# Weights split in two rings of twelve blocks instead of six pairs of blocks: a two-layer decoder trunk on one core

## The chip, the cores and the metric

The kernel runs on one core of one Trainium2 chip. The metric is the device time of one execution in microseconds (us); lower is better. Before the change it is 2327.83 us, the median of three runs (2327.59 to 2328.57).

The engines go by the profile's names: PE is TensorE (matmul; PEld is its weight load), DVE is VectorE, ACT is ScalarE, POOL is GpSimd, SP is SyncE, which issues most of the DMAs.

## The reference

256 tokens of width 2048 pass two pre-norm residual layers. Each layer is a token mixer (layer 0 an HGRN2 gated recurrence, layer 1 gated linear attention) beside a 4-head cross-attention into 256 memory tokens, an output projection, and a SwiGLU feed-forward network of width 5632. All of it is float32.

```python
for layer in range(DEPTH):                      # 2
    hn = _rmsnorm(h, norm_mix[layer])
    if layer % NUM_MIXERS == 0:
        y, xq = _hgrn2_mixer(hn, hgrn_w_in[j], lbs[j], hgrn_onorm[j])
    else:
        y, xq = _gla_mixer(hn, gla_w_in[j], gla_w_gk[j], gla_b_gk[j], gla_onorm[j])
    xa = _memory_attention(xq, mem_n, w_mem_kv[layer])
    h = h + jnp.concatenate([y, xa], axis=-1) @ w_out[layer]
    hn = _rmsnorm(h, norm_ffn[layer])
    gate, up = jnp.split(hn @ w_gate_up[layer], 2, axis=-1)
    h = h + (jax.nn.silu(gate) * up) @ w_down[layer]
return _rmsnorm(h, norm_final)
```

## The kernel before

**Products in two parts.** A float32 factor is split into a high part in the type that the matmul takes (fp32r) and a low part, the rest. A product is three matmuls into one PSUM bank: high x high, high x low, low x high (lines 249 to 251 and 333 to 335). The weights come from memory as float32 and are split on the fly, a block of 128 x 512 at a time: ScalarE copies the block to the high part (line 207), VectorE subtracts the high part from the block and writes the low part (line 208).

**Buffers.** `new_raw` gives one of 4 raw tiles of four blocks (tag "raw"). `split` takes one of 6 tiles of the tag "parts"; each holds the high and low parts of up to two blocks. It is called with one or two blocks. A tile is given back when the last matmul that reads it is done.

**Projections.** `project` walks over quads of 128-row strips of the weights. For each quad `weights` issues one DMA of up to 1 MB and splits it two blocks at a time; then 24 matmuls follow (four strips, two tiles of 128 tokens, three matmuls). The first quad of the program is loaded and split block by block. `step()` places pieces of other work, such as transposes, between the strips.

**Feed-forward.** `ffn` computes gate and up in 11 blocks of 512 columns each (`up_block`), and lays parts of the down projection between them, two `down` calls after each block. `project_halves` does a block: eight pairs of strips, and for each pair a 2 x 2 problem of blocks b00, b01, b10, b11 (strip by half). The kinds of pairs are S, O and H:

- S takes seven products instead of eight. It splits b00, then b11 and b10 together; VectorE forms sums and differences of blocks in place in the raw tile (lines 350 to 352: one instruction of two blocks, two of one); the four results t5, t7 and t6, t4 are split two and two. That makes four tiles of "parts": a (one block), b, c and d (two each). The products go in the order 1, 3, 2, 5, 7, 6, 4. 21 matmuls.
- O takes eight products, 24 matmuls, from two tiles of two blocks.
- H takes eight products; it forms one difference (line 366) and splits it alone, three tiles in all.

Blocks 0 to 2 of a layer have the pairs SHOSHOSO, SHOSSOSO and SHOSSOSO, the other eight SSOSSOSS. After the eighth pair a copy (line 828), additions (line 831), SiLU (line 833) and a product (line 834) follow.

**Order.** Each engine runs its instructions in one order, fixed when the program is made: about that of the source, but an instruction that is found ready early may be put ahead of one that has to wait. Waits between engines go by the part of a tile that is read or written.

**Other tenants.** The keys and values of the cross-attention of both layers (`kv0`, `kv1`), and in layer 1 the reloaded `kv` and the gate's weights and low-rank inputs (`gk`), each take a "parts" tile through `side`.

Of the kernel before, what the change touches and what calls it, by code (L numbers as in the profile page):

```python
# [35 lines left out]
def trunk_kernel(ctx: ExitStack, tc: tile.TileContext, x, mem, norm_mix, norm_ffn, norm_mem,  # L36
# [156 lines left out]
    def side(shape, name):  # L193
        return wts.tile(shape, F32, tag="parts", name=name, bufs=6)

# [5 lines left out]
    def split(src, name, by=2):  # L201

        n, m = src.shape[1:]
        both = wts.tile([P, 2, 2, 512], F32R, tag="parts", name=f"parts{name}", bufs=6)
        for k in range(0, n, by):
            j = min(k + by, n)
            nc.scalar.copy(out=both[:, 0, k:j, 0:m], in_=src[:, k:j, :])  # L207
            nc.vector.tensor_tensor(out=both[:, 1, k:j, 0:m], in0=src[:, k:j, :],  # L208
                                    in1=both[:, 0, k:j, 0:m].bitcast(F32), op=ALU.subtract)
        return [(both[:, 0, k, 0:m], both[:, 1, k, 0:m]) for k in range(n)]  # L210

    def weights(w, k0, nk, c0, n):
# [5 lines left out]
        return [p for k in range(0, nk, 2) for p in split(raw[:, k:k + 2, 0:n], f"{i}_{k}", 1 if i == 0 else 2)]  # L218
# [102 lines left out]
    def project_halves(forms, kinds, w, c0, c1, name):  # L321
# [15 lines left out]
        for p, kind in enumerate(kinds):  # L337
            i, raw = new_raw()

            for j, c in ((slice(0, 4, 3), c0), (slice(1, 3), c1)):  # L340
                nc.sync.dma_start(out=raw[:, j, :],
                                  in_=w[2 * p * P:(2 * p + 2) * P, c:c + 512].rearrange("(k p) c -> p k c", p=P))
            x = forms[p].get
            last = p == len(PAIRS) - 1
            if kind == "S":
                tt = nc.vector.tensor_tensor
                b00, = split(raw[:, 0:1, :], f"{i}a")
                b11, b10 = split(raw[:, 2:4, :], f"{i}b")

                tt(out=raw[:, 0:2, :], in0=raw[:, 0:4:2, :], in1=raw[:, 1:2, :].broadcast_to([P, 2, 512]), op=ALU.subtract)  # L350
                tt(out=raw[:, 2, :], in0=raw[:, 2, :], in1=raw[:, 0, :], op=ALU.add)  # L351
                tt(out=raw[:, 3, :], in0=raw[:, 3, :], in1=raw[:, 2, :], op=ALU.subtract)  # L352
# [108 lines left out]
    kv_out = away.tile([P, 2, XH * T], F32, name="kv_out")  # L461
    later(lambda: nc.scalar.dma_start(out=kv_out, in_=kv))


    def attention(l, ps, r, yq):
# [35 lines left out]
        def turn_probs(m):  # L501
            pT = st["pT", m] = work.tile([P, XH, T], F32, tag=("T", "sc")[m], name=f"pT{l}{m}")
# [260 lines left out]
    def gla(hq, r, yq):  # L763
        w = gla_w_in[0]
        half = (GR + XA) // 2
        kv = side([P, 2, XH * T], "kv")
        nc.scalar.dma_start(out=kv, in_=kv_out)
        kT[1] = kv[:, 0, :].rearrange("p (h t) -> p h t", t=T)
        vm[1] = kv[:, 1, :].rearrange("p (m c) -> p m c", c=XA)
        gk = side([P, 6, T], "gk")  # L770
        wgk = gk[:, 0:4, :]
# [14 lines left out]
        def decay(pr):  # L786
# [3 lines left out]
            for a in range(2):  # L790
                hd = 2 * pr + a
                zp = aux_ps(f"zp{hd}")
                for j in range(2):
                    nc.tensor.matmul(zp[:, j * T:(j + 1) * T], wgk[:, hd, j * P:(j + 1) * P], lowT,
                                     start=True, stop=True)
# [160 lines left out]
```

## Time and profile before

| | |
|---|---|
| median of 3 runs | 2327.83 us |
| the profiled execution | 2328.0 us |
| its span, first to last instruction | 2326.2 us |
| granted TensorE clock | 0.999 |
| busy share PE / DVE / ACT / POOL | 99% / 81% / 54% / 1% |
| DMA | 435.51 MB, mean 187 GB/s |
| feed-forward stage, layer 0 | 544.4 to 1248.1 us |
| feed-forward stage, layer 1 | 1615.9 to 2316.9 us |

The profile is of one execution. The span is shorter than the execution's time by 1.8 us. Matmuls are pipelined and their ends are modelled, so a busy PE isn't PE at its peak; start-to-start times of matmuls say how fast it goes. Instructions of VectorE and ScalarE overlap a little too: the next one can start before the time of the one ahead of it is over, so that start-to-start times are what counts there as well. In a timeline row stand the start, the time, the engine, the line, the operation with output and inputs, and in brackets how long the engine sat idle before it and who released it. The number in a name such as parts152c is the raw tile's number, the letter that of the split.

### The profile page before, as it was taken

To read this page: it belongs to the slowest core of one execution; us is meant where nothing else is said; L and a number is where in the kernel's file an instruction comes from. 1 tells how busy PE (TensorE), PEld (TensorE's weight loads), DVE (VectorE), ACT (ScalarE), POOL (GpSimd) and SP (SyncE) were. 2 spreads that over 40 slices of the span, in tenths; PEclk is the share of its full clock that TensorE was granted. 3 is DMA by queue.
4 is the path that set the end of the run, shared out by engine and by line. 5 is a ranking of instruction groups with operands and counts; after the bars stand their busy time and mean duration, and the time that the engine had idled before them with its cause. 6 is when DMAs were issued, how large, how long until landed. Compare 5 with 4: busy or idle time off the path is not lost.

```text
span 2326.2 us, 28901 instructions
## 1 busy us (share of the span) xinstructions
PE 2303.5 (99%) x11034; PEld 1940.7 (83%) x11034; DVE 1888.0 (81%) x2262; ACT 1261.2 (54%) x1643; POOL 22.2 (1%) x39
## 2 busy tenths in 40 slices
PE   9999999999999999999999999999999999999998
PEld 7888888888887888888889999988887888888886
DVE  5565565668999999999985664557999999999995
ACT  7543535356555655555555654356555555555563
POOL 0000000000000000000000000000000000000000
PEclk9999999999999999999999999999999999999999
DMA  8554445454556555556565445455465656656563
GB/s 315 193 172 159 163 145 181 136 190 164 198 181 214 196 188 202 196 202 209 187 226 166 150 147 167 152 198 174 166 214 189 208 183 209 205 186 213 200 217 127
DMA packets 229211, 435.51 MB, mean 187 GB/s; under 512 B 10028, under 2 KB 38992, under 8 KB 228816
## 3 DMA queue, kind: packets, MB, share of 16 engines
q1 hardware_dynamic: 227776, 429.40, 54.8%
q10 hardware_dynamic: 1296, 4.26, 0.5%
q8 instruction: 86, 1.41, 0.2%
q14 instruction: 53, 0.43, 0.1%
HBM read 430.48 MB, written 3.15 MB: 186 GB/s over the span
## 4 chain that ended last, share of the span: by engine, by line
PE 63%; DVE 26%; issue 6%; ACT 4%; DMA 0%; ACTq 0%; DVEq 0%; POOLq 0%; SPq 0%
PE f_p L334 4%; PE f_p L335 4%; PE f_p L333 4%; DVE raw L350 4%; DVE parts L208 4%; PE fd L250 3%; PE fd L251 3%; PE fd L249 3%; PE wo L251 3%; PE wo L249 3%; PE wo L250 2%; DVE raw L351 2%; DVE raw L352 2%; PE slh L578 1%; PE hgate L249 1%
## 5 line engine op out<-in xcount | busy, mean ns | idle before, releaser
L208 DVE TENSOR_TENSOR parts<-raw,parts 128x1024 fp32r<-128x1024 f32 (+3 forms) x490 | 557.7, 1147 | 290.8 <-ACT parts L207 289.9
L207 ACT CAST parts<-raw 128x1024 fp32r<-128x1024 f32 (+3 forms) x490 | 476.8, 991 | 430.4 <-PE wo L251 64.4
L350 DVE TENSOR_TENSOR raw<-raw 128x1024 f32<-128x1024 f32 x118 | 143.7, 1217 | 0.2
L351 DVE TENSOR_TENSOR raw<-raw 128x512 f32<-128x512 f32 x118 | 81.6, 692 | 3.9
L352 DVE TENSOR_TENSOR raw<-raw 128x512 f32<-128x512 f32 x118 | 81.6, 692 | 3.8
L414 DVE TENSOR_TENSOR h<-fd,h 128x512 f32<-128x512 f32 x94 | 61.9, 684 | 6.2 <-PE fd L251 6.0
L831 DVE TENSOR_TENSOR e<-f_p,e 128x512 f32<-128x512 f32 x66 | 44.9, 681 | 0.0
L833 ACT ACTIVATE s<-s,rf_r 128x512 f32<-128x512 f32 x44 | 31.8, 722 | 7.0 <-DVE s L831 7.0
L562 DVE COPY_PREDICATED sch<-mask,slh 128x512 f32<-128x512 uint8 x15 | 10.8, 722 | 28.4 <-PE slh L578 28.4
L834 DVE SCALAR_TENSOR_TENSOR s<-e,rf_r,s 128x512 f32<-128x512 f32 x44 | 32.3, 741 | 0.0
L578 PEld LDWEIGHTS slh<-Q,K 128*128 128x128 f32 x240 | 29.1, 191 | 1.2
L831 DVE TENSOR_TENSOR s<-f_p,e 128x512 f32<-128x512 f32 x44 | 29.5, 683 | 0.0
L578 PE MATMUL slh<-Q,K 128*128 128x64 f32 x240 | 28.4, 271 | 0.0
L249 PE MATMUL wo<-parts,y_3h 128*128 128x512 f32 x64 | 25.9, 405 | 0.0
L249 PE MATMUL wo<-parts,y_0h 128*128 128x512 f32 x64 | 25.7, 402 | 0.0
L250 PE MATMUL fd<-parts,s_5h 128*128 128x512 f32 x64 | 25.4, 397 | 0.0
L250 PE MATMUL fd<-parts,s_7h 128*128 128x512 f32 x64 | 25.4, 396 | 0.0
L250 PE MATMUL fd<-parts,s_1h 128*128 128x512 f32 x64 | 25.3, 396 | 0.0
L249 PE MATMUL fd<-parts,s_2h 128*128 128x512 f32 x64 | 25.3, 396 | 0.0
L249 PE MATMUL fd<-parts,s_4h 128*128 128x512 f32 x64 | 25.3, 396 | 0.0
L249 PE MATMUL fd<-parts,s_6h 128*128 128x512 f32 x64 | 25.3, 396 | 0.0
L249 PE MATMUL fd<-parts,s_8h 128*128 128x512 f32 x64 | 25.3, 396 | 0.0
(5486 smaller groups left out, 7401.6 us busy)
## 6 DMA issues: line engine op xcount, KB each, us to landing
raw<-in_w_gate_up_dram SPq DMA_DIRECT2D x352, 512.0 KB, 4.0
raw<-in_w_down_dram SPq DMA_DIRECT2D x88, 1024.0 KB, 4.9
raw<-in_hgrn_w_in_dram SPq DMA_DIRECT2D x52, 1024.0 KB, 5.0
raw<-in_gla_w_in_dram SPq DMA_DIRECT2D x48, 768.0 KB, 4.3
raw<-in_w_out_dram SPq DMA_DIRECT2D x32, 1024.0 KB, 4.9
raw<-in_w_mem_kv_dram SPq DMA_DIRECT2D x15, 1024.0 KB, 8.2
raw<-in_gla_w_in_dram SPq DMA_DIRECT2D x8, 528.0 KB, 3.7
mtok<-in_mem_dram SPq DMA_DIRECT2D x4, 512.0 KB
```

The costliest lines, as they stand in the source:

```text
L207: nc.scalar.copy(out=both[:, 0, k:j, 0:m], in_=src[:, k:j, :])
L208: nc.vector.tensor_tensor(out=both[:, 1, k:j, 0:m], in0=src[:, k:j, :], in1=both[:, 0, k:j, 0:m].bitcast(F32), op=ALU.subtract)
L249: nc.tensor.matmul(acc, xh, hi[:, o:o + m], start=first, stop=False)
L250: nc.tensor.matmul(acc, xh, lo[:, o:o + m], start=False, stop=False)
L251: nc.tensor.matmul(acc, xl, hi[:, o:o + m], start=False, stop=last)
L333: nc.tensor.matmul(ps[b], xh, hi, start=first, stop=False)
L334: nc.tensor.matmul(ps[b], xh, lo, start=False, stop=False)
L335: nc.tensor.matmul(ps[b], xl, hi, start=False, stop=left[b] == 0)
L350: tt(out=raw[:, 0:2, :], in0=raw[:, 0:4:2, :], in1=raw[:, 1:2, :].broadcast_to([P, 2, 512]), op=ALU.subtract)
L351: tt(out=raw[:, 2, :], in0=raw[:, 2, :], in1=raw[:, 0, :], op=ALU.add)
L352: tt(out=raw[:, 3, :], in0=raw[:, 3, :], in1=raw[:, 2, :], op=ALU.subtract)
L578: nc.tensor.matmul(ps, st["K"][:, f, t * P:(t + 1) * P], q, start=i == 0, stop=i == len(parts) - 1)
```

## The change

The six "parts" tiles give way to two tiles that are allocated once: `part_h` with the high parts and `part_l` with the low parts of twelve blocks each. `split` takes places in them in turn, round and round, and takes as many neighbouring blocks at once as it is given, so one VectorE instruction writes the low parts of up to four blocks; at the end of the ring it breaks in two. ScalarE's copies still take two blocks (three for the first split of an S pair). The capacity in blocks is what the six tiles had.

For an S pair there are now two splits, of three and of four blocks, where there were four. The raw tile's blocks lie in another order (b00, b11, b10, b01), a pair is loaded by three DMAs instead of two, and the products go 1, 3, 2, 5, 6, 4, 7. An O pair and a quad of `weights` are one split of four. Keys, values and gate inputs move from "parts" tiles to tiles of the "work" pool.

```diff
-        both = wts.tile([P, 2, 2, 512], F32R, tag="parts", name=f"parts{name}", bufs=6)
-        for k in range(0, n, by):
-            j = min(k + by, n)
-            nc.scalar.copy(out=both[:, 0, k:j, 0:m], in_=src[:, k:j, :])
-            nc.vector.tensor_tensor(out=both[:, 1, k:j, 0:m], in0=src[:, k:j, :],
-                                    in1=both[:, 0, k:j, 0:m].bitcast(F32), op=ALU.subtract)
-        return [(both[:, 0, k, 0:m], both[:, 1, k, 0:m]) for k in range(n)]
+    NB = 12
+    part_h = wts.tile([P, NB, 512], F32R, name="part_h")
+    part_l = wts.tile([P, NB, 512], F32R, name="part_l")
+    at = [0]
+    def split(src, by=2):
+        n, m = src.shape[1:]
+        pairs = []
+        k = 0
+        while k < n:
+            i = at[0] % NB
+            j = min(n - k, NB - i, n if by > 1 else 1)
+            at[0] += j
+            hi, lo, s = part_h[:, i:i + j, 0:m], part_l[:, i:i + j, 0:m], src[:, k:k + j, :]
+            for c in range(0, j, by):
+                d = min(c + by, j)
+                nc.scalar.copy(out=hi[:, c:d, :], in_=s[:, c:d, :])
+            nc.vector.tensor_tensor(out=lo, in0=s, in1=hi.bitcast(F32), op=ALU.subtract)
+            pairs += [(hi[:, c, :], lo[:, c, :]) for c in range(j)]
+            k += j
+        return pairs
...
-        return [p for k in range(0, nk, 2) for p in split(raw[:, k:k + 2, 0:n], f"{i}_{k}", 1 if i == 0 else 2)]
+        return split(raw[:, 0:nk, 0:n], 1 if i == 0 else 2)
...
-            for j, c in ((slice(0, 4, 3), c0), (slice(1, 3), c1)):
-                nc.sync.dma_start(out=raw[:, j, :],
-                                  in_=w[2 * p * P:(2 * p + 2) * P, c:c + 512].rearrange("(k p) c -> p k c", p=P))
+            lo, hi = [w[(2 * p + k) * P:(2 * p + k + 1) * P, :] for k in range(2)]
+            nc.sync.dma_start(out=raw[:, 0:4:2, :],
+                              in_=w[2 * p * P:(2 * p + 2) * P, c0:c0 + 512].rearrange("(k p) c -> p k c", p=P))
+            nc.sync.dma_start(out=raw[:, 1, :], in_=hi[:, c1:c1 + 512])
+            nc.sync.dma_start(out=raw[:, 3, :], in_=lo[:, c1:c1 + 512])
...
             if kind == "S":
                 tt = nc.vector.tensor_tensor
-                b00, = split(raw[:, 0:1, :], f"{i}a")
-                b11, b10 = split(raw[:, 2:4, :], f"{i}b")
-                tt(out=raw[:, 0:2, :], in0=raw[:, 0:4:2, :], in1=raw[:, 1:2, :].broadcast_to([P, 2, 512]), op=ALU.subtract)
-                tt(out=raw[:, 2, :], in0=raw[:, 2, :], in1=raw[:, 0, :], op=ALU.add)
-                tt(out=raw[:, 3, :], in0=raw[:, 3, :], in1=raw[:, 2, :], op=ALU.subtract)
-                t5, t7 = split(raw[:, 0:2, :], f"{i}c")
-                t6, t4 = split(raw[:, 2:4, :], f"{i}d")
+                b00, b11, b10 = split(raw[:, 0:3, :], 3)
+                tt(out=raw[:, 0:4:3, :], in0=raw[:, 0:2, :], in1=raw[:, 3:4, :].broadcast_to([P, 2, 512]), op=ALU.subtract)
+                tt(out=raw[:, 1, :], in0=raw[:, 1, :], in1=raw[:, 0, :], op=ALU.add)
+                tt(out=raw[:, 2, :], in0=raw[:, 2, :], in1=raw[:, 1, :], op=ALU.subtract)
+                t5, t6, t4, t7 = split(raw)
...
-                for b in (1, 2, 6, 7, 5, 4, 3) if last else (1, 3, 2, 5, 7, 6, 4):
+                for b in (1, 2, 6, 7, 5, 4, 3) if last else (1, 3, 2, 5, 6, 4, 7):
                     product(b, x(todo[b][0]), todo[b][1])
             else:
-                b00, b01 = split(raw[:, 0:2, :], f"{i}a")
-                b11, b10 = split(raw[:, 2:4, :], f"{i}b")
+                b00, b11, b10, b01 = split(raw)
...
-                    nc.vector.tensor_tensor(out=raw[:, 3, :], in0=raw[:, 3, :], in1=raw[:, 2, :], op=ALU.subtract)
-                    e1, = split(raw[:, 3:4, :], f"{i}c")
+                    nc.vector.tensor_tensor(out=raw[:, 2, :], in0=raw[:, 2, :], in1=raw[:, 1, :], op=ALU.subtract)
+                    e1, = split(raw[:, 2:3, :])
...
-        kv = side([P, 2, XH * T], f"kv{l}")
-        kT.append(kv[:, 0, :].rearrange("p (h t) -> p h t", t=T))
-        vm.append(kv[:, 1, :].rearrange("p (m c) -> p m c", c=XA))
+        kT.append(work.tile([P, XH, T], F32, tag=("v", "F")[l], name=f"kT{l}"))
+        vm.append(work.tile([P, NT, XA], F32, tag=("gate", "K")[l], name=f"vm{l}"))
...
+    def put_away():
+        nc.scalar.dma_start(out=kT_out, in_=kT[1])
+        nc.scalar.dma_start(out=vm_out, in_=vm[1])
...
-        kv = side([P, 2, XH * T], "kv")
-        nc.scalar.dma_start(out=kv, in_=kv_out)
...
+        kT[1] = work.tile([P, XH, T], F32, tag="v", name="kT")
+        nc.scalar.dma_start(out=kT[1], in_=kT_out)
+        vm[1] = work.tile([P, NT, XA], F32, tag="gate", name="vm")
+        nc.scalar.dma_start(out=vm[1], in_=vm_out)
+        both = work.tile([P, 3, T], F32, tag="sc", name="gk0")
+        wgk = [both[:, 0:2, :], work.tile([P, 2, T], F32, tag="scx", name="gk1")]
+        for pr in range(2):
+            nc.gpsimd.memset(wgk[pr], 0.0)
+            nc.sync.dma_start(out=wgk[pr][0:GR, :, 0:DK], in_=gla_w_gk[0][:, 2 * pr * DK:2 * (pr + 1) * DK].rearrange(
+                "r (h c) -> r h c", c=DK))
```

More of the change, by code (lines that the diff above doesn't have):

```diff
@@ L459, in trunk_kernel @@
             nc.scalar.activation(out=vm[l][:, t, :], in_=ps[t], func=AF.Copy, scale=rm[:, t:t + 1])
-    kv_out = away.tile([P, 2, XH * T], F32, name="kv_out")
-    later(lambda: nc.scalar.dma_start(out=kv_out, in_=kv))
+    kT_out = away.tile([P, XH, T], F32, name="kT_out")
+    vm_out = away.tile([P, NT, XA], F32, name="vm_out")
+    def put_away():
+        nc.scalar.dma_start(out=kT_out, in_=kT[1])
+        nc.scalar.dma_start(out=vm_out, in_=vm[1])
+    later(put_away)
     def attention(l, ps, r, yq):
@@ L501, in turn_probs @@
         def turn_probs(m):
-            pT = st["pT", m] = work.tile([P, XH, T], F32, tag=("T", "sc")[m], name=f"pT{l}{m}")
+            pT = st["pT", m] = work.tile([P, XH, T], F32, tag=("T", "Q")[m], name=f"pT{l}{m}")
             for j in range(2):
@@ L778, in gla @@
             nc.scalar.activation(out=low[:, t, 0:GR], in_=psx[0][t][:, 0:GR], func=AF.Copy, scale=r[:, t:t + 1])
-        lowT = gk[:, 5, :]
+        lowT = work.tile([P, T], F32, tag="junk", name="lowT")
         dec = {}
```

13 lines of the change are left out of this document (2 added, 11 removed).

## The prediction

> **What bounds the kernel now.** I read the page first, then busy time by stage, then the timeline of VectorE, ScalarE and TensorE in one steady block of a feed-forward layer.
>
> ```profile
> span 2326.2 us, 28901 instructions
> PE 2303.5 (99%) x11034; PEld 1940.7 (83%) x11034; DVE 1888.0 (81%) x2262; ACT 1261.2 (54%) x1643; POOL 22.2 (1%) x39
> ```
>
> TensorE (PE) is called 99% busy, but the ends of matmuls are modelled, so that figure can't say who waits. Busy time in the two feed-forward stages and in one stretch of the mixers says more (columns: stretch, its length, busy time of PE, its weight load, VectorE, ScalarE and GpSimd, then clock, DMA share, GB/s):
>
> ```profile
> 544.40:1248.10 703.70, 699.70 (x3114) 570.56 (x3113) 669.81 (x758) 400.57 (x474) 1.90 (x3) 1.00 0.58 196
> 1615.90:2316.90 701.00, 697.13 (x3088) 567.77 (x3086) 668.50 (x755) 395.31 (x462) 1.24 (x2) 1.00 0.57 194
> 100.00:150.00 50.00, 50.00 (x231) 41.75 (x230) 28.94 (x40) 24.45 (x38) 0.00 (x0) 1.00 0.58 197
> 550.00:600.00 50.00, 50.00 (x227) 41.31 (x226) 46.98 (x62) 30.25 (x39) 0.00 (x0) 1.00 0.55 185
> 600.00:650.00 50.00, 49.30 (x222) 40.37 (x221) 48.17 (x55) 27.51 (x32) 0.00 (x0) 1.00 0.57 195
> 850.00:900.00 50.00, 49.52 (x221) 40.19 (x220) 49.20 (x57) 28.09 (x32) 0.00 (x0) 1.00 0.61 204
> ```
>
> In the mixers VectorE works 29 of 50 us and PE has no gap. From the fourth feed-forward block on VectorE is busy 49 of 50 us. Which of the two sets the pace there is seen in the timelines (start, time in us, engine, line, output<-inputs, shape, count, idle before). VectorE first, one S pair and its neighbours:
>
> ```profile
> 901.26 1.23 DVE L208 TENSOR_TENSOR parts151d<-raw,parts151d 128x1024 fp32r<-128x1024 f32 x1
> 902.40 0.68 DVE L208 TENSOR_TENSOR parts152a<-raw,parts152a 128x512 fp32r<-128x512 f32 x1
> 903.00 1.22 DVE L208 TENSOR_TENSOR parts152b<-raw,parts152b 128x1024 fp32r<-128x1024 f32 x1
> 904.14 1.22 DVE L350 TENSOR_TENSOR raw<-raw 128x1024 f32<-128x1024 f32 x1
> 905.39 0.69 DVE L351 TENSOR_TENSOR raw<-raw 128x512 f32<-128x512 f32 x1
> 906.11 0.69 DVE L352 TENSOR_TENSOR raw<-raw 128x512 f32<-128x512 f32 x1
> 906.72 1.22 DVE L208 TENSOR_TENSOR parts152c<-raw,parts152c 128x1024 fp32r<-128x1024 f32 x1
> 908.00 1.22 DVE L208 TENSOR_TENSOR parts152d<-raw,parts152d 128x1024 fp32r<-128x1024 f32 x1
> 909.15 1.22 DVE L208 TENSOR_TENSOR parts153a<-raw,parts153a 128x1024 fp32r<-128x1024 f32 x1
> ...
> 922.49 1.22 DVE L208 TENSOR_TENSOR parts155c<-raw,parts155c 128x1024 fp32r<-128x1024 f32 x1
> ...
> 985.67 1.22 DVE L208 TENSOR_TENSOR parts167c<-raw,parts167c 128x1024 fp32r<-128x1024 f32 x1
> 986.81 0.68 DVE L831 TENSOR_TENSOR s<-f_p,e 128x512 f32<-128x512 f32 x1
> 987.41 1.22 DVE L208 TENSOR_TENSOR parts167d<-raw,parts167d 128x1024 fp32r<-128x1024 f32 x1
> ...
> 1048.88 1.22 DVE L208 TENSOR_TENSOR parts179c<-raw,parts179c 128x1024 fp32r<-128x1024 f32 x1
> ```
>
> The S pair 152 runs from 902.40 to 909.15: 6.75 us without a hole. A steady block (eight pairs and four quads of the down projection, twelve raw tiles) takes 985.67-922.49 = 63.18 us, the next one 63.21. Then PE in the same pair, and its transposes:
>
> ```profile
> 902.83 0.39 PE L333 MATMUL f_p<-parts151c,hf_3h 128*128 128x512 f32 x1
> ...
> 905.55 0.39 PE L333 MATMUL f_p<-parts152a,hf_4h 128*128 128x512 f32 x1
> ...
> 908.04 0.48 PE L333 MATMUL f_p<-parts152d,hf_4h 128*128 128x512 f32 x1
> ...
> 910.43 0.39 PE L333 MATMUL f_p<-parts153a,hf_5h 128*128 128x512 f32 x1
> ...
> 935.64 0.82 PE L160 MATMUL tp_s_6h<-ident,s 128*128 128x128 f32 x6
> ```
>
> The first two rows are twelve matmuls apart, 2.72 us, so a matmul costs 0.2267. From 905.55 to 910.43 the 21 matmuls of pair 152 take 4.88 instead of 4.76: PE has caught up and waits for VectorE. PE's own need for a steady block is 6 S pairs of 21 and 2 O pairs of 24 matmuls plus 96 of the down projection, 270 x 0.2267 = 61.2, plus eight transposes at about 0.11, 62.1 us. So VectorE sets the 63.2 us, and PE stands only 1.1 us behind it. That is the most that any relief of VectorE can win: 16 steady blocks (8 in each layer) x 1.1 = 17 us.
>
> **What the change saves on VectorE.** From the rows, start to start: one block of 512 costs 0.60 (986.81 to 987.41), two cost 1.14 (903.00 to 904.14). That is 0.534 a block and 0.07 an instruction; by the same line three cost 1.67 and four 2.20, an estimate, as no row shows such a subtract. An S pair now pays 0.60 + 1.14 + 2.58 (904.14 to 906.72, the three sums) + 1.28 + 1.15 = 6.75. After: 1.67 + 2.58 + 2.20 = 6.45, less by 0.29 and before any wait. An O pair, and a quad of weights(), pays 2.20 for 2 x 1.14: 0.07 less. A steady block saves 6 x 0.29 + 6 x 0.07 = 2.2. A ring of twelve cuts some operations in two where it wraps: walking the places through the code, a feed-forward layer has 238 (layer 0) and 232 (layer 1) subtracts instead of 386, where unbroken ones would be 195; the cuts cost 0.25 us a block. VectorE's own work for a steady block becomes 63.2 - 2.2 + 0.25 = 61.3 us, under PE's 62.1. Left at that, PE would set the pace and all of the 17 us would be won.
>
> The Trainium skill, VectorE: DVE Perf Modes, section "The DRAIN you can't avoid", says that a next operation doesn't start until the pipe is empty; by that an instruction removed would save its whole fixed time, 0.69 - 0.53 = 0.16 instead of 0.07. The trace does not agree: the subtract at 903.00 lasts 1.22 and the next starts 1.14 after it. By the page a steady block (14 subtracts fewer) would come to about 60.0 us on VectorE instead of 61.3; PE's 62.1 would bound it all the same.
>
> **What it adds: a wait in front of the four-block subtract.** ScalarE in the same pair:
>
> ```profile
> 901.13 0.61 ACT L207 CAST parts152a<-raw 128x512 fp32r<-128x512 f32 x1
> 901.64 1.05 ACT L207 CAST parts152b<-raw 128x1024 fp32r<-128x1024 f32 x1
> 905.46 1.05 ACT L207 CAST parts152c<-raw 128x1024 fp32r<-128x1024 f32 x1 [2.77 <-DVE raw L350]
> 906.92 1.06 ACT L207 CAST parts152d<-raw 128x1024 fp32r<-128x1024 f32 x1 [0.40 <-DVE raw L352]
> 907.88 1.04 ACT L207 CAST parts153a<-raw 128x1024 fp32r<-128x1024 f32 x1
> ```
>
> Now the copy of c starts as soon as L350 is done and runs beside L351 and L352; VectorE subtracts c while ScalarE copies d; VectorE waits 0.14 (908.00 instead of 907.86). The halves cover each other. After the change the sums stand so that the first two of the four blocks are final after the second sum and the last two after the third, ScalarE still copies two and two, but one subtract waits for both copies. With the times above: second sum done 905.39+0.69 = 906.08, copy starts 906.19 (the rows show 0.11 from 906.81 to 906.92); third done 906.81; second copy starts behind the first, 0.95 after it (906.92 to 907.88), at 907.14, ends 908.19; the subtract starts at about 908.22. VectorE was free at 906.72: a wait of 1.50 us in every S pair, behind which, on VectorE's queue, everything stands, and PE with it once it has used up what is split. The cover that the old order had, half c under copy d, is what the change merges away.
>
> The order on an engine isn't strictly that of the source: at 986.81 an addition of the block's end stands between c and d, put into just such a hole. So the next pair's first subtract may fill it. How well? If it is an S pair, its three-block copy needs three places of the ring that hold b10, t5 and t6 of the pair before the current one (7 blocks a pair, 12 places). Say that pair's four-block subtract ends at 0. PE, caught up, frees t6 about 1.6 later (two products of 0.68 and the end of the last matmul, 0.39); the copy of three takes about 1.5 (0.61 and 1.05 go up by 0.44 a block) and ends at 3.1; the current pair's two copies, ready at 2.1, queue behind it on ScalarE to about 4.9; VectorE is done with the sums at 2.6, subtracts the next three from 3.1 to 4.8 and the four from 5.0 to 7.2. That is 7.2 a pair, 0.75 of it waiting. If an O pair or a quad follows (3 of the 6 in a block, SSOSSOSS and then the quads), its four-block subtract of 2.2 is longer than the hole and can hide it wholly. So the wait w per S pair lies between 0.4 (all filled as well as the ring allows: half at 0.75, half at 0) and 1.5 (nothing filled). I take 1.0, nearer to the upper end, by the row of 152c: ScalarE idles 2.77 us ahead of it, long enough for two copies of the next pair, and takes none; even the finer ring of halves keeps the next pair's copy late.
>
> The block is then 61.3 + 6 x 1.0 = 67.3, 4.1 more than 63.2; x 16 = 66 us. In the first three blocks of a layer there are 11 S pairs: 11 us of wait, less about 4 saved, less about 6 that VectorE has idle there (3.0 and 1.8 in the two 50 us rows, little after), about 2 us a layer, 4 in all. Sum 70 us.
>
> The Trainium skill, Perfetto Trace Analysis, section "Optimizing Scalar/DVE Operations", has both sides: grouping into larger operations can improve throughput where the engine is saturated, and breaking up instructions may let work complete sooner where they cause bubbles on other engines. The first, taken alone, is the first rival below; no run yet shows a merged subtract.
>
> **Edits at nothing.** In the mixers, the memory projections and the output projections PE has no gap and VectorE idles 21 of 50 us, so a quad's first matmul may wait 1.1 longer for its split: two other quads are in the ring, 5.4 us of matmuls each. Without that cover it would be 1.1 us x some 150 quads; with VectorE's idle time the other bound is nothing won either. A pair loads by three transfers instead of two on SyncE's queue: 176 more issues, no more bytes, with four raw tiles in turn and the DMA share at 0.58; if late, a pair would lose the issue of one transfer. Keys and values of layer 1 go out and back as two transfers each on ScalarE's queue, the gate weights as two on SyncE's with one memset more on GpSimd, all under matmuls of a stage where PE never stops: within 1 us either way. The new order 5, 6, 4, 7 of products only follows the blocks.
>
> **Rivals.** (1) Faster: waits are filled as well as the 0.14 now, VectorE needs 61.3 and PE's 62.1 rules: 2328.0 - 17 = 2311. For it: the filled hole at 986.81, and the ring frees places block by block. Against it: it needs w below (63.2-61.3)/6 = 0.32, and the S-S cycle alone gives 0.75. The skill's rule on grouping speaks for this one. (2) Nothing filled, w = 1.5: 61.3 + 9 = 70.3, 7.1 x 16 = 114, and the early blocks 11 x 1.5 - 10 = 6.5 a layer: 2328 + 127 = 2455. For it: copies and subtracts follow the source order in every row above. (3) About the same: w near 0.35, 2328 to 2334. (4) The ring is tracked as one tile, so that every write waits for all matmuls: a pair would be 6.45 + 1.5 + 4.76 in a row, 6 us more on 118 pairs, 700 us. Against it: the copy at 905.46 reads the tile that L351 and L352 still write, so waits go by the part of a tile.
>
> **The numbers.** The profiled execution took 2328.0 us, 1.8 outside its span, 0.2 from the median 2327.83. Forecast 2328 + 70 = 2398 us (w of 0.7 to 1.3: 2370 to 2428), chance 0.62; nothing filled 0.12; same 0.07; faster 0.18; the whole-tile wait 0.01. The range has to reach both ways: 2316, most of the faster case, to 2448, short of nothing filled. A measurement of this kernel can tell about 0.2%, 4.7 us: faster 0.18, same 0.07, slower 0.75.
>
> **What would show it.** Subtracts of 2048 columns at 2.2 start to start; about 470 subtracts in the two feed-forward layers; holes of 0.5 to 1.5 us on VectorE ahead of the four-block subtract after L352's successor, released by ScalarE's copy; PE's matmul pitch still 0.227 but holes in it; a steady block of 65 to 69 us; the mixers unchanged. It is wrong if the block comes to 62.1 with VectorE under 98% busy (rival 1), or if the subtracts of four cost clearly more than 2.3.

## The result and the profile after

The changed kernel takes 2409.31 us, the median of four runs (2408.54 to 2415.99), against 2328.2 for the kernel before beside it: ratio 1.0355, 95% interval 1.0336 to 1.0373. It is 81 us slower; the forecast was 70 slower. The profiled execution took 2409.39 us.

From the page of the changed kernel, the span, the engines and the costliest group of VectorE (line, engine, operation, tiles, count | busy, mean ns | idle before, and its releaser):

```profile
span 2407.5 us, 28622 instructions
...
PE 2327.5 (97%) x11034; PEld 1939.7 (81%) x11034; DVE 1851.2 (77%) x1829; ACT 1265.0 (53%) x1607; POOL 27.4 (1%) x40
...
L217 DVE TENSOR_TENSOR part_l<-raw,part_h 128x2048 fp32r<-128x2048 f32 (+6 forms) x653 | 1142.1, 1769 | 360.8 <-ACT part_h L216 358.8
```

VectorE has 433 instructions fewer and is busy for a smaller share of a longer span. The subtract is now line 217, the copy to the high part line 216, the three sums of an S pair lines 361 to 363. Busy time by stage, the two feed-forward stages first, then one stretch of the mixer and one of a steady part (columns as before):

```profile
545.00:1296.90 751.90, 713.09 (x3114) 570.14 (x3113) 660.34 (x612) 402.33 (x460) 3.04 (x3) 1.00 0.55 185
1665.20:2399.40 734.20, 707.89 (x3088) 567.47 (x3086) 657.86 (x603) 393.12 (x419) 2.81 (x2) 1.00 0.55 185
100.00:150.00 50.00, 50.00 (x232) 41.70 (x230) 26.91 (x31) 24.06 (x37) 0.00 (x0) 1.00 0.59 198
850.00:900.00 50.00, 45.50 (x193) 35.94 (x192) 45.09 (x41) 26.02 (x28) 0.00 (x0) 0.97 0.67 230
```

The stages grew from 1404.7 to 1486.1 us, by 81.4: all of the loss. Span less stages is 921.5 before and 921.4 after, so nothing happened in the mixers and projections, where PE still has no gap. In the stages VectorE's busy time fell from 1338.3 to 1318.2 (-20.1), and the time in which it does nothing (length less busy) rose from 33.9 + 32.5 = 66.4 to 91.6 + 76.3 = 167.9 (+101.5). PE, which had 0.5 us of holes in the 50 us from 850, has 4.5 now. VectorE does less and waits more. The subtracts alone in the two stages:

```profile
545.00:1296.90 751.90, 407.56 (x239) 1.00 0.55 185
1665.20:2399.40 734.20, 403.61 (x230) 1.00 0.55 185
```

Where it waits is seen in its timeline in layer 0 (start, time, engine, line, tiles, shape, count, idle before and releaser):

```profile
904.23 0.69 DVE L362 TENSOR_TENSOR raw<-raw 128x512 f32<-128x512 f32 x1
904.95 0.69 DVE L363 TENSOR_TENSOR raw<-raw 128x512 f32<-128x512 f32 x1
907.06 3.96 DVE L217 TENSOR_TENSOR part_l<-raw,part_h 128x2048 fp32r<-128x2048 f32 x2 [1.41 <-ACT part_h L216]
...
929.67 1.23 DVE L361 TENSOR_TENSOR raw<-raw 128x1024 f32<-128x1024 f32 x1
930.84 2.29 DVE L217 TENSOR_TENSOR part_l<-raw,part_h 128x2048 fp32r<-128x2048 f32 x1
933.05 0.68 DVE L362 TENSOR_TENSOR raw<-raw 128x512 f32<-128x512 f32 x1
...
940.05 0.69 DVE L363 TENSOR_TENSOR raw<-raw 128x512 f32<-128x512 f32 x1
942.30 2.29 DVE L217 TENSOR_TENSOR part_l<-raw,part_h 128x2048 fp32r<-128x2048 f32 x1 [1.56 <-ACT part_h L216]
945.18 1.76 DVE L217 TENSOR_TENSOR part_l<-raw,part_h 128x1536 fp32r<-128x1536 f32 x1 [0.59 <-ACT part_h L216]
...
961.03 1.75 DVE L217 TENSOR_TENSOR part_l<-raw,part_h 128x1536 fp32r<-128x1536 f32 x1
962.70 0.69 DVE L847 TENSOR_TENSOR e<-f_p,e 128x512 f32<-128x512 f32 x1
```

And ScalarE beside the first of these holes:

```profile
905.03 2.00 ACT L216 CAST part_h<-raw 128x1024 fp32r<-128x1024 f32 x2 [3.94 <-DVE raw L362]
907.39 1.49 ACT L216 CAST part_h<-raw 128x1536 fp32r<-128x1536 f32 x1 [0.37 <-PE fd L261]
```

The first copy starts 0.11 after the second sum's end (904.92), the two copies end at 907.03, and the subtract of four blocks starts at 907.06: a hole of 1.41 us, with 1.56 in another pair. At 930.84 a four-block subtract of other work stands between the first and the second sum, and no hole follows the third. At 942.30 the next pair's three-block subtract could not fill the hole: its own copy was late as well, and it waits 0.59 more. The four-block subtracts of the two stages, layer 0 and then layer 1 (columns as in the first list):

```profile
L217 DVE TENSOR_TENSOR part_l<-raw,part_h 128x2048 fp32r<-128x2048 f32 x103 | 234.9, 2287 | 54.4 <-ACT part_h L216 54.3
...
L217 DVE TENSOR_TENSOR part_l<-raw,part_h 128x2048 fp32r<-128x2048 f32 x95 | 216.3, 2286 | 37.0 <-ACT part_h L216 37.0
```

The holes ahead of them come to 91 us, but these 198 subtracts are not all of S pairs: O pairs and quads have four blocks too. Counted in the trace, 72 of the 91 us stand directly behind a third sum, nearly all in 46 holes of 1.34 us and more, most of them about 1.4. Where the ring cuts an S pair's four blocks, the piece behind the third sum has another 12 us. Together that is 84 us, 0.71 for each of the 118 S pairs.

### The profile page after: what moved, and what is told of

The parts are those of the page before. It is cut to its first block, busy times and chain, and to the rows that moved or that the text cites. A ratio compares the mean times of both kernels' runs of the same rounds, so it can differ in the third digit from the quotient of the medians.

```text
span 2407.5 us, 28622 instructions
## 1 busy us (share of the span) xinstructions
PE 2327.5 (97%) x11034; PEld 1939.7 (81%) x11034; DVE 1851.2 (77%) x1829; ACT 1265.0 (53%) x1607; POOL 27.4 (1%) x40
## 3 DMA queue, kind: packets, MB, share of 16 engines
q8 instruction: 86, 1.41, 0.2%
## 4 chain that ended last, share of the span: by engine, by line
PE 83%; DVE 9%; issue 4%; ACT 3%; DMA 1%; DVEq 0%; ACTq 0%; POOLq 0%
PE f_p L344 9%; PE f_p L343 9%; PE f_p L345 9%; PE fd L260 6%; DVE part_l L217 6%; PE fd L261 6%; PE fd L259 6%; ACT part_h L216 3%; PE wo L261 2%; PE wo L259 2%; PE wo L260 2%; PE slh L592 1%; PE hgate L259 1%; PE gv L259 1%; PE ggate L259 1%
## 5 line engine op out<-in xcount | busy, mean ns | idle before, releaser
L216 ACT CAST part_h<-raw 128x1024 fp32r<-128x1024 f32 (+5 forms) x1050 | 1022.0, 1000 | 966.2 <-PE f_p L345 204.8
L217 DVE TENSOR_TENSOR part_l<-raw,part_h 128x2048 fp32r<-128x2048 f32 (+6 forms) x653 | 1142.1, 1769 | 360.8 <-ACT part_h L216 358.8
L344 PE MATMUL f_p<-part_l,hf_5h 128*128 128x512 f32 x176 | 70.9, 403 | 3.1 <-DVE part_l L217 2.9
L344 PE MATMUL f_p<-part_l,hf_2h 128*128 128x512 f32 x176 | 69.6, 395 | 1.3 <-DVE part_l L217 1.3
L345 PE MATMUL f_p<-part_h,hf_5l 128*128 128x512 f32 x176 | 69.2, 394 | 0.0
L345 PE MATMUL f_p<-part_h,hf_2l 128*128 128x512 f32 x176 | 69.2, 394 | 0.0
L343 PE MATMUL f_p<-part_h,hf_2h 128*128 128x512 f32 x176 | 66.8, 396 | 0.5 <-ACT part_h L216 0.5
L343 PE MATMUL f_p<-part_h,hf_5h 128*128 128x512 f32 x176 | 66.4, 394 | 0.1
L344 PE MATMUL f_p<-part_l,hf_1h 128*128 128x512 f32 x160 | 63.6, 397 | 1.4 <-DVE part_l L217 1.4
L345 PE MATMUL f_p<-part_h,hf_1l 128*128 128x512 f32 x160 | 62.6, 391 | 0.0
```

The costliest lines, as they stand in the source:

```text
L216: nc.scalar.copy(out=hi[:, c:d, :], in_=s[:, c:d, :])
L217: nc.vector.tensor_tensor(out=lo, in0=s, in1=hi.bitcast(F32), op=ALU.subtract)
L343: nc.tensor.matmul(ps[b], xh, hi, start=first, stop=False)
L344: nc.tensor.matmul(ps[b], xh, lo, start=False, stop=False)
L345: nc.tensor.matmul(ps[b], xl, hi, start=False, stop=left[b] == 0)
```

## The experiments

The theory after the result: the merged subtract has to wait for both of ScalarE's copies, and that wait is the loss. The rivals: the new order of products and the wide copies keep places of the ring too long; the places at which the ring wraps cut the work badly; TensorE is slower by itself. The edits are against the changed kernel, unless another is named.

### The wait taken away, or made longer (e1, e2, e3, e4)

e1 keeps every size and lets the four-block subtract of an S pair read the block itself, so that it needs no copy (the low part of these blocks is then zero, and a part of the product is left out).

```diff
-    def split(src, by=2):
+    def split(src, by=2, free=False):
...
-            nc.vector.tensor_tensor(out=lo, in0=s, in1=hi.bitcast(F32), op=ALU.subtract)
+            nc.vector.tensor_tensor(out=lo, in0=s, in1=s if free else hi.bitcast(F32), op=ALU.subtract)
...
-                t5, t6, t4, t7 = split(raw)
+                t5, t6, t4, t7 = split(raw, free=True)
```

> The changed kernel, but the four-block subtract of an S pair takes the raw block from itself, so that it no longer needs the copies (the low part of these four blocks is zero, which leaves out a part of the product). Same sizes, same ring, same copies. Theory (the wait for both copies in front of that subtract costs the time): the holes of 1.4 us go, the two feed-forward stages come back from 752 and 734 us to 700-712, the whole to 2315-2345 us. Rival A (the ring of twelve gives its places back too late for pieces of three and four; the wait is only where it shows): holes move to the copies and PE, 2380 us or more. Rival B (the extra DMAs, the new places of keys and values, the order of products): 2409 as it is.

Measured: 2355.63 us (ratio to the kernel before 1.0114, 1.0097 to 1.0131). 54 of the 81 us are gone with the same instructions. Its stages:

```profile
545.20:1255.40 710.20, 702.78 (x3114) 569.17 (x3113) 661.50 (x612) 402.36 (x460) 5.39 (x3) 1.00 0.59 195
1623.50:2345.30 721.80, 702.28 (x3088) 569.80 (x3086) 658.34 (x603) 396.08 (x419) 1.24 (x2) 1.00 0.56 188
```

VectorE's work is about the same, 1319.8; its idle time is 112.2 instead of 167.9. In this run the trace tells the S pairs' subtracts apart, as they have no `part_h` among their inputs. The ring leaves the four blocks of 76 of the 118 S pairs whole, and 5 us of holes are left ahead of them:

```profile
L217 DVE TENSOR_TENSOR part_l<-raw 128x2048 fp32r<-128x2048 f32 x76 | 174.0, 2289 | 5.1 <-DVE raw L363 0.5
```

e2 gives the four results of an S pair back their two splits of two, and leaves the first three blocks, the O pairs and the quads merged:

```diff
-                t5, t6, t4, t7 = split(raw)
+                t5, t7 = split(raw[:, 0:4:3, :])
+                t6, t4 = split(raw[:, 1:3, :])
...
-                for b in (1, 2, 6, 7, 5, 4, 3) if last else (1, 3, 2, 5, 6, 4, 7):
+                for b in (1, 2, 6, 7, 5, 4, 3) if last else (1, 3, 2, 5, 7, 6, 4):
```

> The changed kernel with the second split of an S pair made as two splits of two blocks again, t5 with t7 and t6 with t4, and the old order of products 5, 7, 6, 4; ring, loads, the first split of three and the splits of four of O pairs and quads stay. Theory: half c covers copy d again, a steady block needs about 62.5 us on VectorE, 2315-2335 us in all. Rival A: smaller pieces help a ring of any cause, 2330-2380. Rival B: 2409.

Measured: 2350.79 us (1.0095, 1.008 to 1.011), 58.5 under the changed kernel. e3 goes the other way: one copy of four blocks, which can start only after the third sum.

```diff
-                t5, t6, t4, t7 = split(raw)
+                t5, t6, t4, t7 = split(raw, 4)
```

> The changed kernel with one ScalarE copy of four blocks in place of two of two ahead of the four-block subtract. The copy can only start after the third sum: by the rows 0.11 + 1.9 + 0.03 after it instead of 1.41, a wait of about 2.0 us. Theory: slower by 0.4-0.6 us on each S pair whose hole isn't filled, 96 pairs in steady blocks: 2430-2455 us. Rivals A and B: the ring and the loads are as they were, 2400-2415.

Measured: 2448.13 us (1.0506, 1.0489 to 1.0523), 39 more than the changed kernel. The holes ahead of four-block subtracts come to 128 us instead of 91. At most 14 of the 39 us can be TensorE's clock, which was at half for 41 us instead of 14 (the last section comes to that). Take the wait away and the time falls, lengthen it and it grows. e4 only shifts the ring by one place, and so changes which pairs are cut where it wraps:

```diff
-    at = [0]
+    at = [1]
```

> The changed kernel with the ring's first place moved on by one, so that layer 0 of the feed-forward meets the ring as layer 1 did in the changed kernel (layer 1 then starts at place 2). Nothing else. Theory: a four-block subtract that the ring's end cuts in two is a half that covers a copy, and layer 1 had more of them (43 pieces of two blocks against 17); layer 0's stage falls from 752 to 732-738 us, the whole by 10-25 us. If places don't matter and layer 0 is slow for another reason, its stage stays at 752 and the whole at 2409.

Measured: 2393.64 us (1.0279, 1.0263 to 1.0294), 16 less, from 751.9 to 740.1 us in layer 0. So the place of the cuts matters, but much less than the wait. Layer 0 has 43 subtracts of two blocks instead of 17, and six subtracts fewer in all; layer 1 has 19 more and is not slower (733.5 instead of 734.2). That a cut helps because it lets a part of a split go early fits this, but is not shown by itself.

e1 and e2 leave about 25 us that the wait for both copies doesn't explain. Both came out above what the theory gave them, and e2 lies in the range of the first rival, pieces too large for the ring. The trace of e1 agrees: with the one wait gone, the holes ahead of three-block subtracts in the two stages grew from 19 to 36 us.

### Which merge costs what (e5, e6, e7, e9, e10, e12)

e6 keeps the ring, the new loads and places, and merges nothing:

```diff
-        return split(raw[:, 0:nk, 0:n], 1 if i == 0 else 2)
+        return [p for k in range(0, nk, 2) for p in split(raw[:, k:k + 2, 0:n], 1 if i == 0 else 2)]
...
-                b00, b11, b10 = split(raw[:, 0:3, :], 3)
+                b00, = split(raw[:, 0:1, :])
+                b11, b10 = split(raw[:, 1:3, :])
...
-                t5, t6, t4, t7 = split(raw)
+                t5, t7 = split(raw[:, 0:4:3, :])
+                t6, t4 = split(raw[:, 1:3, :])
...
-                for b in (1, 2, 6, 7, 5, 4, 3) if last else (1, 3, 2, 5, 6, 4, 7):
+                for b in (1, 2, 6, 7, 5, 4, 3) if last else (1, 3, 2, 5, 7, 6, 4):
...
-                b00, b11, b10, b01 = split(raw)
+                b00, b11 = split(raw[:, 0:2, :])
+                b10, b01 = split(raw[:, 2:4, :])
```

> The ring, the loads by three transfers and the new places of keys and values alone: every split takes one or two blocks as in the kernel before (S pair 1, 2, 2, 2; O pair and quad 2, 2). Theory C: no merge, no new wait, 2310-2330 us; a difference to e5_first12 is what the merges of four are worth, at most 0.07 us x 5.5 subtracts x 22 blocks = 8 us. Theory D: 2325-2330 here but 2345-2355 in e5_first12. Theory E: 2345-2355 here too.

The others put one or more of these hunks back as the changed kernel has them: e7 only the split of three, e9 only the split of the four results (with its order of products), e12 only the quads of weights(), e5 the O pairs and the quads, e2 those and the split of three. e10 is e5 with the four-block subtract of e1, which waits for no copy.

> The kernel of e2_half57 (second split of an S pair by halves, 2351 us) with the first split of an S pair as one block and two again; O pairs and quads stay at one split of four. It asks what the 22 us are that e2_half57 and e1_nowait (27) still lack. Theory C: a piece of three needs three neighbouring places of the ring free at once, so its one copy is late and VectorE waits ahead of the 1536-wide subtract (22 and 25 us of holes there in e2_half57 and e1_nowait, both layers together): these go and the time comes to 2310-2330 us, at or below the kernel before. Theory D (the splits of four of O pairs and quads cost it): 2345-2355, as e2_half57. Theory E (ring, loads, new places of keys and values): 2345-2355 as well.

> As e6_ring_by2, but the first split of an S pair takes three blocks at once: the only merge is this one. Theory C: it brings back most of the 22 us of e2_half57, 2335-2350 us. Theory D: it costs nothing, within 5 us of e6_ring_by2.

> The kernel of e6_ring_by2 (2312 us) with one merge: the second split of an S pair as one of four (products in the changed kernel's order 5, 6, 4, 7). Theory (the wait for both copies): this merge alone brings most of the loss, the holes of 1.4 us are back, 2355-2385 us. If the merges only hurt together, because the ring is then cut into large pieces everywhere: 2312-2330.

> e1_nowait (the four-block subtract doesn't need the copies; the low part of those four blocks is zero, which leaves out a part of the product) with the first split of an S pair as one and two blocks. If the wait and the piece of three are the whole of the loss, merges of four that don't wait cost nothing: 2311-2320 us. If something else is left in the pieces of four: 2325-2345.

> e6_ring_by2 with one merge: quads of the projections as one split of four (in the mixers too); O and S pairs in ones and twos. e5_first12, with O pairs and quads merged, is 5 us slower than e6_ring_by2. If the quads cost it: 2315-2318 us; if the O pairs do, or both together: 2311-2314. In the mixers nothing changes in any case (921 to 922 us outside the feed-forward stages).

| kernel | merged | us | ratio to before (95%) | against e6 |
|---|---|---|---|---|
| e6 | nothing | 2311.95 | 0.9931 (0.9918 to 0.9943) | 0 |
| e12 | quads | 2314.17 | 0.9936 (0.9924 to 0.9949) | +2 |
| e5 | O pairs, quads | 2316.94 | 0.995 (0.9936 to 0.9963) | +5 |
| e10 | as e5, and four results without the wait | 2318.02 | 0.9954 (0.9942 to 0.9967) | +6 |
| e7 | first three | 2328.23 | 1.0 (0.9991 to 1.0009) | +16 |
| e9 | four results | 2344.24 | 1.0068 (1.0054 to 1.0082) | +32 |
| e2 | first three, O pairs, quads | 2350.79 | 1.0095 (1.008 to 1.011) | +39 |
| changed kernel | all | 2409.31 | 1.0355 (1.0336 to 1.0373) | +97 |

Four things follow. The loads, the new places of keys and values and the ring as such are not the loss: e6 has them all. No merge gains; the split of three and that of the four results cost, while the 2 to 6 us of e12, e5 and e10 lie at the edge of what the intervals can tell. e10 against e5 (+1) says that the merged subtract without its wait costs next to nothing, and wins nothing either; e10 has the new order of products 5, 6, 4, 7 and e5 the old one, so that order isn't the loss. And the costs don't add up: 16 + 32 + 5 = 53, all together 97. e9, for which 2355 to 2385 was expected, shows it from one side: alone, with small pieces about it, the four-block split costs 32; with large ones (e2 to the changed kernel) 58.5. The split of three costs 16 among small pieces, less than was expected for e7, and 34 among large ones (e5 to e2). Before e6 and e5 ran, the merges of four were expected to win up to 8 us; e5 is 5 slower than e6. e12's 2 us are too few to tell quads from O pairs.

### Why the ring alone wins 16 us (e8, e11)

e6 was not expected by the prediction: same blocks and sizes as the kernel before, 45 VectorE instructions more in the stages (cuts of the ring), and 16 us faster. Its stages, then the engines in one S pair (lines 362 to 364 are the sums here), VectorE and then ScalarE:

```profile
545.80:1241.00 695.20, 695.12 (x3114) 571.38 (x3113) 662.74 (x789) 406.99 (x504) 2.52 (x3) 1.00 0.59 199
1608.80:2302.40 693.60, 693.60 (x3088) 568.30 (x3086) 659.89 (x769) 400.82 (x476) 2.29 (x2) 1.00 0.58 195
```

```profile
908.38 1.21 DVE L362 TENSOR_TENSOR raw<-raw 128x1024 f32<-128x1024 f32 x1
909.52 0.68 DVE L217 TENSOR_TENSOR part_l<-raw,part_h 128x512 fp32r<-128x512 f32 x1
910.12 0.68 DVE L363 TENSOR_TENSOR raw<-raw 128x512 f32<-128x512 f32 x1
910.72 1.23 DVE L217 TENSOR_TENSOR part_l<-raw,part_h 128x1024 fp32r<-128x1024 f32 x1
911.86 0.69 DVE L364 TENSOR_TENSOR raw<-raw 128x512 f32<-128x512 f32 x1
```

```profile
908.61 0.62 ACT L216 CAST part_h<-raw 128x512 fp32r<-128x512 f32 x1 [2.54 <-PE f_p L345]
909.63 1.06 ACT L216 CAST part_h<-raw 128x1024 fp32r<-128x1024 f32 x1 [0.40 <-DVE raw L362]
```

The copy of one block at 908.61 belongs to the next pair and goes ahead of the current pair's copies; its subtract stands between two sums. The rows of the kernel before in the prediction have copies and subtracts in the order of the source. e11 is e6, and e8 the changed kernel, with each copy bound behind the copy before it in the source:

```diff
+    prev = [None]
...
-                nc.scalar.copy(out=hi[:, c:d, :], in_=s[:, c:d, :])
+                if prev[0] is None:
+                    ins = nc.scalar.copy(out=hi[:, c:d, :], in_=s[:, c:d, :])
+                else:
+                    with tc.issue_after(prev[0]):
+                        ins = nc.scalar.copy(out=hi[:, c:d, :], in_=s[:, c:d, :])
+                prev[0] = ins.ins
```

> The kernel of e6_ring_by2 with ScalarE's copies of weights bound to the order of the source. It asks why the ring by itself is 16 us faster than the six tiles. Theory F (with the tiles the copies stood in the order of the source, and with the ring the next pair's copy may go ahead): back to 2322-2332 us. Theory G (an S pair takes seven places instead of the eight of four tiles, so there is more room): 2310-2316.

> The changed kernel with ScalarE's copies of weights bound to the order of the source, as they stood in the kernel before; nothing else. It asks how much of the wait of 1.4 us the next pair's early copy hides in the changed kernel. Theory (the wait, filled in part): without early copies every S pair waits the whole 1.4-1.5 us, and the first rows of O pairs and quads wait as well: 2450-2510 us. If the holes are not filled now either: 2409.

e11: 2332.73 us (1.0017, 1.0008 to 1.0026). Bound to the old order, the ring's gain is gone, and 4 us more. Its stages, and VectorE in one S pair (sums 368 to 370):

```profile
544.60:1252.60 708.00, 701.09 (x3114) 569.78 (x3113) 673.30 (x789) 401.40 (x504) 2.02 (x3) 1.00 0.58 195
1620.40:2322.30 701.90, 697.58 (x3088) 567.41 (x3086) 668.81 (x769) 392.09 (x476) 1.79 (x2) 1.00 0.57 193
```

```profile
905.99 1.22 DVE L368 TENSOR_TENSOR raw<-raw 128x1024 f32<-128x1024 f32 x1
907.24 0.69 DVE L369 TENSOR_TENSOR raw<-raw 128x512 f32<-128x512 f32 x1
907.97 0.69 DVE L370 TENSOR_TENSOR raw<-raw 128x512 f32<-128x512 f32 x1
```

This shows where the time comes from. A sum that reads what the sum before it wrote starts 1.25 and 0.73 us after it (905.99, 907.24, 907.97); with another pair's subtract between, the steps are 1.14 and 0.60 (e6 at 908.38, 909.52, 910.12). Counted in the trace, the second sum stands directly behind the first in 112 of 118 S pairs of e11 and in 29 of e6, the third directly behind the second in 111 and in 17. These 177 steps at 0.11 to 0.13 are about 21 us. VectorE's busy time in the stages is 1342.1 in e11 and 1322.6 in e6, 19.5 less for the same 1558 instructions, while its idle time is 67.8 and 66.2; the stages differ by 21.1. So the order of ScalarE's copies is worth 20 us, and it is won on VectorE. That the kernel before keeps the source order because its six tiles are handed out in that order is argued from its code; its trace has the sums directly one behind the other as e11 has (110 and 112 of 118). Shown is that the order carries the gain.

e8: 2491.79 us (1.0701, 1.0687 to 1.0716). With the same merges and hardly a hole filled, 82 more than the changed kernel. The stages:

```profile
545.80:1338.20 792.40, 746.49 (x3114) 581.11 (x3113) 668.18 (x612) 394.91 (x460) 2.02 (x3) 0.97 0.52 175
1706.50:2485.80 779.30, 732.87 (x3088) 571.18 (x3086) 666.30 (x603) 385.33 (x419) 1.79 (x2) 0.98 0.51 175
```

VectorE is idle for 124.2 + 113.0 = 237.2 us, 171 more than before the change. Of this 132 us stand directly behind third sums: 72 four-block subtracts wait there, as a rule 1.41 us, and pieces that the ring has cut wait less. Its work is 1334.5, only 3.8 under that of the kernel before.

## Why the prediction was right in direction, and where it failed

**The bound.** That VectorE sets the pace and PE stands 17 us behind it held: e6, with 16 us less work on VectorE, reaches 2312, the 2311 of the first rival, and there PE has no hole (695.12 of 695.20 us).

**The sizes.** Four blocks were to cost 2.20 start to start and cost 2.21 (930.84 to 933.05); three were to cost 1.67 and cost 1.67 (961.03 to 962.70). About 470 subtracts were forecast, 469 are there. The prediction set a sentence of the Trainium skill (VectorE: DVE Perf Modes, section "The DRAIN you can't avoid") against a row that starts early. The section itself goes on that a next operation that is not held starts earlier, and here the independent ones do, by 0.08 us.

**The wait.** 1.50 us if unfilled was forecast, counted from the moment at which VectorE could have gone on, 0.08 before the third sum's end. From that end it is 1.42, and that is what the rows of the changed kernel and of e8 show (most often 1.41 or 1.42). That other work can fill it and that an S pair fills it badly is seen at 930.84 and 945.18. e1, e2 and e3 show that it is the main cause.

**The sum.** Written as idle and work, the forecast was 118 waits of 1.0, less 12 of idle time in the early blocks and 17 of small waits already there (the 0.14 in each pair), +89 of idle time; and 302 instructions x 0.07, -21 of work. Measured: +101.5 and -20.1. The idle term was 12 too small, nearly all of the 11 us that were missing. But it is made up otherwise: the waits behind third sums came to 0.71 a pair instead of 1.0, and 27 us stand where the sum had nothing, ahead of VectorE's other instructions (13.6 us before, 40.8 after), mostly additions that wait for a result of PE. Blocks in the steady part, from one first product of line 850 to the next, took 67.8 to 69.9 us in layer 0 and 63.7 to 70.8 in layer 1, against 65 to 69 forecast.

**Right for partly wrong reasons.** Three steps failed:

- "Even the finer ring of halves keeps the next pair's copy late", read from ScalarE's 2.77 us of idle time. It was mainly the order of the copies: e6 against e11. A full ring delays them too (2.54 us ahead of the copy at 908.61 in e6), but in e6 that copy still comes in time to stand between the sums. The prediction therefore gave the ring itself nothing, and it is worth 16 us. Of this part of the change the profile before showed the sign (idle ScalarE, copies strictly in source order) and the prediction drew the wrong cause from it.
- "A steady block saves": the merges were credited with 0.07 us an instruction. Merging 343 subtracts took 1322.6 to 1318.2 us, 4.4 (e6 to the changed kernel), and 7.6 in source order (e11 to e8), where 24 would follow. The -20.1 that agreed so well is mostly the freer order: e8, with the same merges in source order, has -3.8. Where the rest of the saving went can be counted in the traces. The instructions' own times add up to 1439.6 us in e11 and 1387.3 in e8, 52 less, 0.15 for each instruction merged away. But of this 0.08 had cost nothing before, as it lay under the next instruction, and an instruction ahead of a hole or of one that reads its result shows its whole time (0.69 at 940.05 instead of 0.60): 1174 instructions of e11 are overlapped by their successor, and 662 of e8. The overlap falls from 97.6 to 53.0 us, and 7.6 are left. From e6 to the changed kernel it is 47.9 less of own time against 43.4 less of overlap.
- The merge of the first three blocks was counted as a saving alone. It costs 16 us alone (e7) and 34 beside merged O pairs and quads (e2 against e5). Its copy needs three neighbouring places free and its subtract the whole copy, as at 945.18; that this is the mechanism is argued from such rows, and no run took that wait apart.

So the total came out close by luck: a gain that wasn't seen (the order of the copies) stood against costs that weren't seen (the piece of three, the waits for PE, the saving that stayed away), and w itself was too large by 0.3.

**The rivals.** "Nothing filled" (2455) is e8: 2492. Its unfilled wait was right (above); 17 of the missing 37 us are work that the merges didn't save, and the rest is idle time outside the term. How much of that comes from TensorE's lower clock (below) was not taken apart. Whole-tile tracking did not occur. The mixers were unchanged, as forecast.

The Trainium skill, Perfetto Trace Analysis, section "Optimizing Scalar/DVE Operations", advises larger operations where an engine is saturated. VectorE was saturated here, and by the table above no merge gained. Breaking up instructions so that work completes sooner is what the section gives for engines that are not saturated; the prediction left that condition out. In this case the smaller pieces were faster on a saturated engine.

**What stays open.** Why merges cost 97 together and 53 apart. Larger pieces fill a hole worse and need more of the ring at once, and the rows agree with that; but the two remaining combinations (four results with the first three, four results with O pairs and quads) weren't run.

**A better version.** e6, the ring with the old sizes, takes 2311.95 us: 0.9931 of the kernel before (0.9918 to 0.9943), 0.7% faster than that and 4% faster than the changed kernel.

## What to carry to other kernels

A merged instruction starts when its last input is there and gives nothing until it ends; where two engines work on halves in turn, price the lost overlap (here up to 1.5 us a pair) before the saved overhead (0.07 an instruction, and 0.01 to 0.02 in fact). Where an engine idles while work for it seems ready, ask whether the order in which its instructions were laid down holds it, and test that with an experiment that changes only the order. When a change has several parts, run each alone: here one part that nobody costed was a gain of 16 us, and none of the parts that were meant to gain did.

## What the runs showed of the hardware

**Dependent instructions on VectorE.** An instruction that reads the result of the one before it starts 0.03 after that one's end (905.99 + 1.22 to 907.24); one that doesn't starts 0.08 before the end (909.52 + 0.68 to 910.12). That is 0.11 us a step, and it was worth 20 us here.

**The granted clock fell to half after some short holes, and not after others.** In the changed kernel the mean clock by core is 0.996, in e8 0.982, against 0.999 before. Two stretches of the changed kernel of 3.4 us at clock 0.50, then TensorE's rows ahead of them:

```profile
896.30:899.70 3.40, 3.05 (x10) 2.46 (x11) 2.75 (x5) 0.39 (x1) 0.00 (x0) 0.50 0.52 199
...
1831.50:1834.90 3.40, 3.40 (x10) 2.63 (x9) 2.80 (x3) 0.00 (x0) 0.00 (x0) 0.50 0.85 280
```

```profile
896.65 0.69 PE L160 MATMUL tp_s_5h<-ident,s 128*128 128x128 f32 x2 [2.48 <-DVE s L850]
...
897.56 0.63 PE L260 MATMUL fd<-part_l,s_3h 128*128 128x512 f32 x1
897.99 0.63 PE L261 MATMUL fd<-part_h,s_3l 128*128 128x512 f32 x1
...
1828.24 0.51 PE L343 MATMUL f_p<-part_h,hf_2h 128*128 128x512 f32 x1 [0.30 <-ACT part_h L216]
1829.18 0.74 PE L343 MATMUL f_p<-part_h,hf_1h 128*128 128x512 f32 x2 [0.44 <-ACT part_h L216]
1830.86 0.50 PE L344 MATMUL f_p<-part_l,hf_2h 128*128 128x512 f32 x1 [0.95 <-DVE part_l L217]
```

After a hole of 2.48 us a matmul takes 0.43 (897.56 to 897.99) instead of 0.227, for 3.4 us. Ahead of the stretch at 1831.5 no hole was longer than 0.95 us; it followed three within 3 us. The changed kernel has four such stretches in its feed-forward layers, a loss of at most 4 x 1.7 = 7 us, and that is all that the rival of a slower TensorE can have; e8 has 20 of 3.4 or 6.8 us, 85 us together, and at mean clocks of 0.97 and 0.98 its stages lose roughly 24 + 16 us of clock. But a longer hole of the changed kernel left the clock as it was, and the matmuls behind it go at 0.23:

```profile
1170.80 0.44 PE L160 MATMUL tp_s_9h<-ident,s 128*128 128x128 f32 x2 [3.31 <-DVE s L850]
...
1171.31 0.39 PE L260 MATMUL fd<-part_l,s_7h 128*128 128x512 f32 x1
1171.54 0.39 PE L261 MATMUL fd<-part_h,s_7l 128*128 128x512 f32 x1
```

Four more holes of 2.48 or 2.49 us were not followed by the half clock either. The four stretches start at 759.74, 896.28, 1831.53 and 1916.86, that is 40, 274 and 25 times 3.4133 us apart. So the place of a hole on a grid of 3.4133 us seems to count, and not its length alone; no run tests that.

The Trainium skill, TensorE: Matmul & The Clock Gate, section "Why this matters for your kernels", says to leave no idle gaps over about 3 us between bursts of matmuls. Here holes of 2.48 us, and of 0.95 us in a row of smaller ones, were followed by the half clock, and one of 3.31 us wasn't, so the page's bound isn't what decided.
